# Buffers that are 32 bytes longer, and a smaller scratch for software DMAs, in a two-layer hybrid encoder on one core

## The chip, the cores and the metric

The kernel runs on one core of one Trainium2 chip. The metric is the device time of one execution in microseconds (us). Three executions of the kernel before took 2349.69 us at the median, between 2348.4 and 2352.19 us. One further execution was recorded by the profiler; it took 2351.57 us, of which its trace covers 2349.8 us from the first to the last instruction.

## The reference

The reference computes two layers of an encoder on one sequence of 512 tokens with a model width of 1024, all in fp32:

```python
for l in range(DEPTH):                       # 2 layers
    xn = rmsnorm(x, norm1_g[l])
    h = xn @ w_in[l]
    (a_qkv, a_z, a_ab, b_q, ..., d_o) = jnp.split(h, offsets, axis=-1)
    y_a = gdn_mixer(a_qkv, a_z, a_ab, ...)   # gated DeltaNet
    y_b = diff_mixer(b_q, b_k, b_v, ...)     # differential attention
    y_c = swa_mixer(c_q, c_k, c_v, ...)      # windowed attention
    y_d = mlstm_mixer(d_q, d_k, d_v, ...)    # mLSTM
    ys = jnp.stack([y_a, y_b, y_c, y_d], axis=2)
    branch = jnp.einsum('bsnw,nwd->bsnd', ys, w_branch[l])
    gate = jax.nn.sigmoid(jnp.einsum('bsd,dne->bsne', xn, w_gate[l]))
    x = x + jnp.sum(gate * branch, axis=2) @ w_out[l]
    xn = rmsnorm(x, norm2_g[l])
    x = x + jnp.square(jax.nn.relu(xn @ w_mlp1[l])) @ w_mlp2[l]
return rmsnorm(x, final_norm_g)
```

The large products with `w_in`, `w_gate`, `w_branch`, `w_out`, `w_mlp1` and `w_mlp2` take most of the time of the matrix engine; the four mixers are many small operations.

## The kernel before

**Products in three passes.** Every large operand v is held as two fp32r tiles, hi (a rounded copy of v, made by ScalarE) and lo (v minus hi, made by VectorE); `split` (L221 to L223) does it for activations and `emit_split` (L282 to L294) for weights. A product is then three matmuls per 128-deep step: hi times hi, hi times lo, lo times hi. Such a group of three is called a triple below. Each matmul loads a block of 128 x 128 as its stationary operand and streams 256 or 512 columns of the other operand, the moving one, through it.

**Where the operands lie.** Tiles come from pools of equally long buffers that lie behind one another in SBUF. Three pools matter here.

- `bg` has 13 buffers of 8,320 bytes per partition (L142, 2080 fp32 words of which 2048 are used). It holds the normalized activations (`xh`, `xl`), the mixers' outputs (`yh`, `yl`), the merged branches (`mh`, `ml`), the hidden layer of the MLP (`hh`, `hl`), the weights of the last MLP product (`twh`, `twl`), unsplit MLP weights (`wq`) and most large tiles of the mixers.
- `wp` has three buffers of 4,096 bytes each for `wh` and for `wl`, the split weights (L288, L289), and two of 4,096 bytes for `wr`, the weights as they come from memory.
- `ar` has 26 buffers of 2,080 bytes for tiles of 512 words, `xsh` and `xsl` of the MLP among them.

The start addresses follow from the order in which the pools are laid out behind a 16,384-byte scratch for software DMAs at address 0. In remainders by 256 bytes, all buffers of `wh`, `wl` and `wr` start at 160. The `bg` buffers start at 224 (buffers 0, 2, 4, ..., 12) or at 96 (buffers 1, 3, ..., 11). The `ar` buffers start at 160, 192, 224, 0, 32 and so on, a step of 32 from one to the next. The last `bg` buffer ends 416 bytes below the end of what the kernel may use. Which `bg` buffer a tile gets follows from the order in which the pool's buffers come free in the program.

**The products' forms.** In `run_a` (L374) the weights are the moving operand, 256 columns wide, and the activations are stationary; it serves the projections (on `xh`, `xl`), the first three quarters of the output projection (on `mh`, `ml`) and the second MLP product M2 (on `hh`, `hl`). M2 takes one pair `hh`, `hl` through four items in a row, one for each 256 columns of the output: 4 x 16 triples or 192 matmuls. `tail_item` (L682) has the same form for the last group of M2, with its weights in `bg`. `run_b` (L400) and `run_b2` (L415) have the weights stationary and 512 columns of `xh`, `xl` or `yh`, `yl` moving. The first MLP product, `M1` (L790), has the weights stationary and 256 columns moving, of `xh`, `xl` in `bg` for some factors and of `xsh`, `xsl` in `ar` for the others. `wo_last` (L741) and `m1_first` (L781) are small variants.

**Order.** The large products form one stream of items in a fixed order. `Item.get` looks ahead: it issues loads of weights on SyncE's queue up to five entries ahead (`emit_dma`, 512 KB each), and splits one or more entries ahead. A driver mixes this stream on TensorE with the small products of the mixers in the stretches 150 to 860 us and 1310 to 2020 us; the MLPs run nearly alone in 860 to 1185 us and from 2020 us to the end.

**Software DMAs.** `late_consts` (L199 to L203) issues six casting DMAs for constants from GpSimd near the start; all other loads and stores named here go through hardware queues.

Of the kernel before, what the change touches and what calls it, by code (L numbers as in the profile page):

```python
# [11 lines left out]
F32R = mybir.dt.float32r  # L12
# [5 lines left out]
P = 128  # L18
# [95 lines left out]
def encoder(ctx: ExitStack, tc: tile.TileContext, a: dict, out: bass.AP, dbg: dict = None):  # L114
    nc = tc.nc
# [5 lines left out]
    wp = ctx.enter_context(tc.tile_pool(name="wp", bufs=3))  # L121
    sp = ctx.enter_context(tc.tile_pool(name="sp", bufs=8))
    ar = ctx.enter_context(tc.tile_pool(name="ar", bufs=NAR))
    bg = ctx.enter_context(tc.tile_pool(name="bg", bufs=NBG))
# [5 lines left out]
    def nm(s):  # L130
        cnt[0] += 1
        return f"{s}_{cnt[0]}"
# [6 lines left out]
        return t[:, :S], t[:, S:2 * S]  # L139

    def B(dt=F32, s="b", w=2048):
        return bg.tile([P, 2080], dt, tag="bg", name=nm(s))[:, :w]  # L142

    def B4(dt=F32, s="b"):
        return B(dt, s).rearrange("p (k c) -> p k c", k=4)
# [10 lines left out]
    def f(ap):  # L156
        return ap.bitcast(F32)
# [24 lines left out]
    def x_load(src, between=None):  # L182
        b = [B(s="x") for _ in range(2)]
        xs = [[b[tt // 2][:, (tt % 2) * DM + h * S:(tt % 2) * DM + (h + 1) * S] for h in range(2)] for tt in range(NT)]
        for tt in range(NT):
            for h in range(2):
                nc.sync.dma_start(xs[tt][h], src[tt * P:(tt + 1) * P, h * S:(h + 1) * S])
            if between is not None:
                between(tt)
        return xs, [t.rearrange("p (t c) -> p t c", t=2) for t in b]  # L190
# [46 lines left out]
    class Item:  # L237
# [6 lines left out]
        def get(self, k):  # L244
            i = self.i0 + k
            last = len(loads) - 1
            la = G['la'] if self.label[:2] in ("m1", "m2") else 1
            while ns_[0] <= min(i + la, last):
                stage(np_, ns_[0], emit_pre)
                emit_split(ns_[0])  # L250
                ns_[0] += 1
            stage(np_, min(i + 2 + la, last), emit_pre)
            stage(nd, min(i + 5, last), emit_dma)
            return wt.pop(i)
# [27 lines left out]
    def emit_split(i):  # L282
        w = loads[i]
        raw = w["src"]() if "src" in w else raws.pop(i)
        if "dest" in w:
            wh, wl = w["dest"]()
        else:
            wh = wp.tile([P, w["kt"], w["nc"]], F32R, tag="wh", name=nm("wh"))  # L288
            wl = wp.tile([P, w["kt"], w["nc"]], F32R, tag="wl", name=nm("wl"))  # L289
        n = w["kt"] // G["sp"]  # L290
        for k in range(0, w["kt"], n):
            act.copy(wh[:, k:k + n], raw[:, k:k + n])  # L292
            dve.tensor_tensor(wl[:, k:k + n], raw[:, k:k + n], f(wh[:, k:k + n]), op=ALU.subtract)  # L293
        wt[i] = (wh, wl)  # L294
# [228 lines left out]
    def build(l, L):  # L523
# [5 lines left out]
        def z_evac(hp):  # L529
            def evac(tp, bank):  # L530
                if hp == 0 and tp == 0:
                    L.zs = B(s="zs").rearrange("p (t c) -> p t c", t=NT)
                d = L.zs[:, 2 * tp:2 * tp + 2, hp * 256:(hp + 1) * 256]
                b3 = bank.rearrange("p (t c) -> p t c", t=2)
                act.activation(d, b3, AF.Tanh, scale=0.5)
                dve.scalar_tensor_tensor(d, d, 1.0, b3, op0=ALU.add, op1=ALU.mult)
                for u in range(2):
                    d4 = d[:, u].rearrange("p (h c) -> p h c", h=2)
                    pool.tensor_tensor(d4, d4, bmid(L.gnh[:, 0, :], 2), op=ALU.mult)
            return evac  # L540
# [1210 lines left out]
```

## Time and profile before

| | before |
|---|---|
| median of three executions | 2349.69 us |
| profiled execution, device time | 2351.57 us |
| its span in the trace | 2349.8 us |
| outside the span | 1.8 us |
| TensorE (PE) busy | 2285.3 us, 97%, 16,992 matmuls |
| weight load (PEld) busy | 2083.2 us, 89% |
| VectorE (DVE) busy | 1582.2 us, 67% |
| ScalarE (ACT) busy | 1187.5 us, 51% |
| GpSimd (POOL) busy | 747.6 us, 32% |
| granted TensorE clock, mean | 0.996 |

TensorE's busy time nearly fills the span, so the sum of the times that its instructions take is nearly the time of the kernel. The duration which the profile gives for one matmul overlaps with that of the next one, since matmuls are pipelined; the pace of a row of matmuls is read from the time between their starts, or from a window that begins and ends with a row of them. A window's matmul count includes those that are still in flight at its start, so that it is a few above the number that started in it. [...]

### The profile page before, as it was taken

How to read it: one execution, taken by the hardware profiler on the slowest of the kernel's cores; microseconds unless marked ns; L12 is line 12 of the kernel's file. 1: busy time of each engine (PE TensorE's matmuls, PEld its weight loads, DVE VectorE, ACT ScalarE, POOL GpSimd, SP SyncE). 2: the span in 40 equal slices, each digit the busy share in tenths (PEclk: the TensorE clock that was granted, in tenths of full speed). 3: DMA queues.
4: the chain of work that ended last, by engine and by line, in shares of the span. 5: the costliest groups of instructions: out<-in, count | busy, mean ns of one | idle time of the engine just before them, and what ended most of it. 6: DMA issues, size and time to landing. Idle time of an engine off the chain costs nothing. (4 is left out here: it accounts for less than half of the span.)

```text
span 2349.8 us, 43335 instructions
## 1 busy us (share of the span) xinstructions
PE 2285.3 (97%) x16992; PEld 2083.2 (89%) x16992; DVE 1582.2 (67%) x2988; ACT 1187.5 (51%) x2777; POOL 747.6 (32%) x806
## 2 busy tenths in 40 slices
PE   7999999999999999999999999999999999999998
PEld 6879987989888989999987799879898889899998
DVE  5774547685786477677767745587767854867775
ACT  4565444654665264344445654365546643534443
POOL 1135552132232134343200555412313310434341
PEclk9999999999999999999999999999999999999999
DMA  6322131222122523333323112321221234233322
GB/s 149 99 46 64 55 95 57 60 88 80 51 71 74 160 71 122 95 109 108 111 74 90 55 55 64 91 63 52 93 82 55 72 106 131 90 97 109 99 82 90
DMA packets 234779, 200.72 MB, mean 85 GB/s; under 512 B 31696, under 2 KB 223824, under 8 KB 234576
## 3 DMA queue, kind: packets, MB, share of 16 engines
q1 hardware_dynamic: 231408, 192.75, 27.5%
q10 hardware_dynamic: 2304, 4.20, 0.5%
q8 instruction: 133, 2.18, 0.4%
q0 software_dynamic: 864, 1.02, 0.2%
q14 instruction: 70, 0.57, 0.1%
HBM read 190.04 MB, written 8.39 MB: 84 GB/s over the span
## 5 line engine op out<-in xcount | busy, mean ns | idle before, releaser
L293 DVE TENSOR_TENSOR wl<-wr,wh 128x512 fp32r<-128x512 f32 x540 | 400.4, 762 | 183.4 <-ACT wh L292 176.1
L292 ACT CAST wh<-wr 128x512 fp32r<-128x512 f32 x540 | 317.0, 621 | 219.0 <-PE pd L436 59.2
L392 PE MATMUL pd<-wh,xh 128*128 128x256 f32 x960 | 279.4, 291 | 0.0
L393 PE MATMUL pd<-wl,xh 128*128 128x256 f32 x960 | 269.8, 281 | 0.0
L394 PE MATMUL pd<-wh,xl 128*128 128x256 f32 x960 | 269.4, 281 | 0.0
L394 PE MATMUL pd<-wh,hl 128*128 128x256 f32 x896 | 248.2, 277 | 0.0
L392 PE MATMUL pd<-wh,hh 128*128 128x256 f32 x896 | 248.0, 277 | 0.0
L393 PE MATMUL pd<-wl,hh 128*128 128x256 f32 x896 | 248.0, 277 | 0.0
L292 ACT CAST wh<-wq 128x512 fp32r<-128x512 f32 x196 | 115.3, 619 | 220.4 <-PE pd L394 94.0
L435 PE MATMUL pd<-xh,wh 128*128 128x512 f32 (+1 forms) x544 | 217.7, 401 | 0.5 <-ACT xh L222 0.5
L436 PE MATMUL pd<-xl,wh 128*128 128x512 f32 (+1 forms) x544 | 209.0, 384 | 1.8 <-DVE xl L223 1.6
L437 PE MATMUL pd<-xh,wl 128*128 128x512 f32 (+1 forms) x544 | 208.8, 384 | 0.0
L293 DVE TENSOR_TENSOR wl<-wq,wh 128x512 fp32r<-128x512 f32 x196 | 181.9, 962 | 13.4 <-ACT wh L292 13.3
L393 PEld LDWEIGHTS pd<-wl,xh 128*128 128x128 f32 x960 | 181.9, 189 | 1.4
L392 PEld LDWEIGHTS pd<-wh,xh 128*128 128x128 f32 x960 | 181.5, 189 | 1.4
L394 PEld LDWEIGHTS pd<-wh,xl 128*128 128x128 f32 x960 | 181.3, 189 | 0.2
L809 POOL TENSOR_TENSOR wq<-wq,wq 128x512 f32<-128x512 f32 x84 | 124.4, 1488 | 163.1 <-DVE wl L293 153.7
L393 PEld LDWEIGHTS pd<-wl,hh 128*128 128x128 f32 x896 | 168.2, 188 | 0.0
L394 PEld LDWEIGHTS pd<-wh,hl 128*128 128x128 f32 x896 | 168.2, 188 | 0.0
L392 PEld LDWEIGHTS pd<-wh,hh 128*128 128x128 f32 x896 | 168.1, 188 | 0.0
L677 DVE TENSOR_TENSOR x<-pd,x 128x512 f32<-128x512 f32 x124 | 85.1, 689 | 101.4 <-PE pd L394 101.4
L1011 POOL TENSOR_TENSOR r<-r,r 128x512 f32<-128x512 f32 (+1 forms) x28 | 35.5, 1266 | 325.8 <-DVE r L1010 185.9
(394 smaller groups left out, 6656.9 us busy)
## 6 DMA issues: line engine op xcount, KB each, us to landing
wr<-in_w_in SPq DMA_DIRECT2D x92, 512.0 KB
wr<-in_w_mlp SPq DMA_DIRECT2D x72, 512.0 KB
wr<-in_w_gate SPq DMA_DIRECT2D x64, 512.0 KB
wq<-in_w_mlp SPq DMA_DIRECT2D x56, 512.0 KB
wr<-in_w_branch SPq DMA_DIRECT2D x32, 512.0 KB
wr<-in_w_out SPq DMA_DIRECT2D x16, 512.0 KB
x<-in_x SPq DMA_DIRECT2D x16, 256.0 KB
gsd<-gs ACTq DMA_DIRECT2D x16, 256.0 KB
```

The costliest lines, as they stand in the source:

```text
L292: act.copy(wh[:, k:k + n], raw[:, k:k + n])
L293: dve.tensor_tensor(wl[:, k:k + n], raw[:, k:k + n], f(wh[:, k:k + n]), op=ALU.subtract)
L392: mm(o, th, wh[:, k4, :], start=(kt == 0 and tt % 2 == 0), stop=False)
L393: mm(o, th, wl[:, k4, :], start=False, stop=False)
L394: mm(o, tl, wh[:, k4, :], start=False, stop=(kt == kts - 1 and tt % 2 == 1))
L435: mm(o, w1_, xh[kt][:, sl], start=(kt == 0 and hi_ == 0), stop=False)
L436: mm(o, w1_, xl[kt][:, sl], start=False, stop=False)
L437: mm(o, w2_, xh[kt][:, sl], start=False, stop=last)
L677: dve.tensor_tensor(d, bank.rearrange("p (t c) -> p t c", t=2), d, op=ALU.add)
L809: pool.tensor_tensor(d[:, k:k + 2], x[:, k:k + 2], y[:, k:k + 2], op=op)
L1011: pool.tensor_tensor(v(t1), v(t1), v(t2), op=ALU.add)
```

## The change

Three places are edited. The buffers of `bg` become 2088 words (8,352 bytes) long, and those of `wh` and `wl` become 1032 words (4,128 bytes); of each the same 2048 or 1024 words are used as before. The scratch for software DMAs at the start of SBUF becomes 4,096 bytes instead of 16,384. The 19 longer buffers need 608 bytes more than before.

```diff
     def B(dt=F32, s="b", w=2048):
-        return bg.tile([P, 2080], dt, tag="bg", name=nm(s))[:, :w]
+        return bg.tile([P, 2088], dt, tag="bg", name=nm(s))[:, :w]
...
-            wh = wp.tile([P, w["kt"], w["nc"]], F32R, tag="wh", name=nm("wh"))
-            wl = wp.tile([P, w["kt"], w["nc"]], F32R, tag="wl", name=nm("wl"))
+            wh, wl = [wp.tile([P, 1032], F32R, tag=t, name=nm(t))[:, :1024].rearrange("p (k c) -> p k c", k=w["kt"])
+                      for t in ("wh", "wl")]
...
-    nc = bacc.Bacc("TRN2", target_bir_lowering=False, num_devices=1)
+    nc = bacc.Bacc("TRN2", target_bir_lowering=False, num_devices=1, dynamic_dma_scratch_size=4096)
```

After it, in remainders by 256 bytes, the three buffers of `wh` start at 160, 192 and 224, those of `wl` at 0, 32 and 64, and the `bg` buffers at 160, 192, 224, 0, 32 and so on, a step of 32 from one to the next. The `ar` buffers all move by the same amount and keep their steps. No instruction is added or removed, and no size of an operand changes.

## Rows read from the trace of the kernel before

**Rows 1.** The page's first part: busy time, share and instructions of each engine.
```profile
PE 2285.3 (97%) x16992; PEld 2083.2 (89%) x16992; DVE 1582.2 (67%) x2988; ACT 1187.5 (51%) x2777; POOL 747.6 (32%) x806
```
**Rows 2.** TensorE's longest waits: line, releaser, us in total, times, longest us.
```profile
PE pm L487 <- DVE nj L472: 15.9, 10, 8.9
PE pm L834 <- DVE wl L293: 5.7, 2, 2.9
```
**Rows 3.** Windows of the two MLPs: us, busy of PE, PEld, DVE, ACT, POOL, clock, DMA.
```profile
860.00:1185.00 325.00, 322.12 (x2753) 321.13 (x2752) 235.87 (x324) 143.69 (x260) 125.55 (x97) 0.99 0.33 103
...
2020.00:2345.00 325.00, 320.04 (x2719) 319.37 (x2717) 227.40 (x312) 136.66 (x247) 123.34 (x95) 0.99 0.30 95
```
**Rows 4.** Groups of TensorE's instructions by form: line, tiles, count, busy, mean ns.
```profile
L392 PE MATMUL pd<-wh,xh 128*128 128x256 f32 x960 | 279.4, 291 | 0.0
...
L392 PE MATMUL pd<-wh,hh 128*128 128x256 f32 x896 | 248.0, 277 | 0.0
...
L435 PE MATMUL pd<-xh,wh 128*128 128x512 f32 x480 | 198.7, 414 | 0.0
...
L832 PE MATMUL pm<-xsh,wh 128*128 128x256 f32 x448 | 126.1, 282 | 0.0
...
L406 PE MATMUL pd<-xh,wh 128*128 128x512 f32 x304 | 121.3, 399 | 0.0
...
L435 PE MATMUL pd<-yh,wh 128*128 128x512 f32 x256 | 104.8, 410 | 0.0
...
L832 PE MATMUL pm<-xh,wh 128*128 128x256 f32 x336 | 95.3, 283 | 0.0
...
L392 PE MATMUL pd<-wh,mh 128*128 128x256 f32 x192 | 53.3, 278 | 0.0
...
L718 PE MATMUL pd<-twh,hh 128*128 128x256 f32 x128 | 36.2, 283 | 0.0
```
**Rows 5.** TensorE's windows of M2, 192 matmuls each: us, PE busy, clock, DMA, GB/s.
```profile
888.53:910.34 21.81, 21.81 (x194) 1.00 0.33 97
2045.83:2068.44 22.61, 22.61 (x194) 1.00 0.30 94
...
2255.60:2278.21 22.61, 22.61 (x194) 1.00 0.34 112
2298.05:2319.83 21.78, 21.78 (x194) 1.00 0.45 138
```
**Rows 6.** TensorE's timeline in a fast and a slow window of M2: start, us, line.
```profile
902.18 0.28 PE L392 MATMUL pd<-wh,hh 128*128 128x256 f32 x1
...
902.52 0.28 PE L392 MATMUL pd<-wh,hh 128*128 128x256 f32 x1
...
2050.07 0.28 PE L392 MATMUL pd<-wh,hh 128*128 128x256 f32 x1
...
2050.43 0.28 PE L392 MATMUL pd<-wh,hh 128*128 128x256 f32 x1
```
**Rows 7.** TensorE's windows of `run_a` on xh (48 matmuls) and mh (192, 288).
```profile
554.67:560.11 5.44, 5.44 (x50) 1.00 0.06 9
572.78:578.43 5.65, 5.65 (x51) 1.00 0.44 134
802.30:824.06 21.76, 21.76 (x195) 1.00 0.33 97
1947.20:1981.28 34.08, 34.08 (x289) 1.00 0.32 101
```
**Rows 8.** TensorE's windows of M1 (24, 72, 24 matmuls) and `tail_item` (93).
```profile
1124.07:1126.89 2.82, 2.82 (x27) 1.00 0.00 0
1126.89:1135.41 8.52, 8.52 (x74) 1.00 0.01 2
1135.41:1138.24 2.83, 2.83 (x26) 1.00 0.17 43
2331.27:2342.34 11.07, 11.07 (x96) 1.00 0.23 84
```
**Rows 9.** TensorE's windows of products 512 columns wide, 12 matmuls each.
```profile
49.10:51.87 2.77, 2.77 (x13) 1.00 0.20 59
51.87:54.68 2.81, 2.81 (x14) 1.00 0.09 17
861.34:864.10 2.76, 2.76 (x13) 1.00 0.03 6
```
**Rows 10.** GpSimd's timeline around the software DMAs: start, us, line, idle before.
```profile
20.51 0.76 POOL L201 DMA_DIRECT2D c_identr<-in_ident  x1
...
23.40 0.54 POOL L201 DMA_DIRECT2D c_swnegr<-in_swneg  x1
36.33 0.96 POOL L551 MEMSET wr<- 128x1024 f32 x1 [12.39 <-DVE wl L293]
```
**Rows 11.** Line 201's DMAs, issue to landing, and the first reader of their constants.
```profile
DMA to landing us min/median/max: 2.8/3.7/6.0
...
L1264 PE MATMUL pm<-c_negr,c_identr x32: 389/448/503, 133.9 to 1462.2; 128*128 128x512 f32 x32
```

## The prediction

> **What bounds the kernel now.** The page's busy times come first: TensorE is busy for 2285.3 of 2349.8 us, and no other engine is above 67% apart from the weight loads, which belong to TensorE [rows 1]. So the time is the sum of what TensorE's instructions take plus some 65 us in which it does nothing. Second, its waits: the largest kind sums to 15.9 us, the next to 5.7 us [rows 2], and the edit touches no wait. Third, the windows by stage: in both MLPs TensorE is busy for 322 of 325 and 320 of 325 us [rows 3]. What an edit of addresses can change is therefore the pace at which matmuls follow one another, and the transfers if these lost time. Fourth, the groups by form give the counts that a change of pace is multiplied with [rows 4]; their mean durations overlap and are no pace.
>
> The pace I read from windows that hold nothing but one row of matmuls. M2 gives the cleanest case: one pair hh, hl, 192 matmuls of 128x256, or 64 triples, and there are 896/64 = 14 such windows. Eleven take 21.76 to 21.82 us, three take 22.61 us [rows 5]; two of each kind are shown. The granted clock is 1.00 in all of them, TensorE has no gap, and the share of DMA is as high in a quick one (0.45) as in a slow one (0.34). The starts show the same step by step: 902.18 to 902.52 us is 340 ns for a triple, 2050.07 to 2050.43 us is 360 ns, about the 353 ns that 22.61/64 gives [rows 6]. Following the order in which bg's buffers are handed out, the three slow windows are those in which both hh and hl lie in odd buffers, at 96 by 256 bytes; in the eleven quick ones at least one of them starts at 224. The weights start at 160 in all. So the pace hangs on where the operands begin. The projections agree: with xh, xl in buffers 11 and 10, 48 matmuls take 5.44 us (340 ns a triple), with 9 and 1, both odd, 5.65 us (353 ns) [rows 7]. The offsets are not the whole story: the output projection ran at 340 ns in layer 0 (21.76/64) and at 355 ns in layer 1 (34.08/96) with hi odd and lo even in both [rows 7].
>
> [...]
>
> **The change part by part.** No instruction, wait, queue entry or size is added or removed. What moves is where wh, wl and bg begin against each other. Before, a weight buffer and a bg buffer always differ by 64 more than a multiple of 128 bytes (160 against 224 or 96). Afterwards wh at 160, 192, 224, wl at 0, 32, 64 and bg in steps of 32 differ by 0, 32, 64 or 96 by 128 about equally often, and wh and wl differ among themselves. Only one relation in four is the present one. For the other three the trace of before has two near rows. The weights of `tail_item` lie in bg as its activations do, so that they differ by 0 by 128: 11.07 us for 31 triples is 357 ns, in the form of `run_a` [rows 8]. And xsh, xsl in ar already stand in steps of 32 against the weights: M1 on them takes 8.52/24 = 355 ns, beside 2.82/8 = 352.5 and 2.83/8 = 354 ns with the same weights and xh in bg [rows 8]. No row of M1 shown reaches 340, with either pool. I price a triple afterwards at 3/4 x 355 + 1/4 x 340 = 351 ns. The ends are 340 (the quickest row of its width) and 357 (the slowest of these); I take a value near the upper end because both rows with another relation lie there.
>
> - *M2, 896 triples [rows 4].* Now 11 x 21.79 + 3 x 22.61 = 307.5 us. Afterwards 896 x 0.351 = 314.5 us: +7.0. Ends: 896 x 0.340 = 304.6 (-2.9) and 896 x 0.357 = 319.9 (+12.4).
> - *`run_a` on xh and mh, 960 + 192 = 1152 triples [rows 4].* The four windows give 340, 353, 340 and 355 ns [rows 7], 347 at equal weight. Afterwards 351: 1152 x 4 ns = +4.6. Ends: 1152 x (340 - 347) = -8.1 and 1152 x (357 - 347) = +11.5. In the stretch with the mixers the stream shares TensorE with small products, but TensorE is busy there too, so a slower triple lengthens the stretch by itself.
> - *M1, 448 + 336 = 784 triples, and the tail, 128 [rows 4].* They stand at 352.5 to 357 ns now [rows 8] and stay there: 0. Ends: 912 x (340 - 355) = -13.7 and 912 x 2 ns = +1.8.
> - *512 columns, 480 + 304 + 256 = 1040 triples [rows 4].* Four triples take 2.76, 2.77 or 2.81 us [rows 9], 690 to 702 ns a triple; the windows do not favour a relation, since 2.77 and 2.81 stand in one item. Taken as 0, with the middle of the rows at 695 as what holds before and after. Ends: 1040 x (690 - 695) = -5.2 and 1040 x 7 ns = +7.3.
> - *Small products of the mixers.* Their operands move by the same steps. They are short and most wait for other engines, and no row tells them apart by address: 0, inside the ends above.
> - *VectorE, ScalarE, GpSimd.* They read and write the moved buffers too, but have at least 33% of idle time [rows 1]; in the MLP window VectorE is busy 235.87 of 325 us and GpSimd 125.55 [rows 3]. Nothing of them is late next unless they slow by a third.
> - *The smaller scratch.* Its users are six DMAs that GpSimd issues between 20.51 and 23.94 us, one every 0.5 us without waiting for a landing of 2.8 to 6.0 us [rows 10, 11]. Afterwards 0 at best. At worst each issue waits for the landing before it, 6 x 6.0 = 36 us instead of 3.4, so that GpSimd is free at 56.5 instead of 23.9 us; 12.39 us of that lie in the idle time ahead of the memset at 36.33 us, which comes 20 us late [rows 10]. The constants' first reader comes at 133.9 us [rows 11], so they would land in time, and only the memsets behind them on GpSimd would be late. I take 0.
>
> **The sum.** 7.0 + 4.6 + 0 = 11.6 us on the profiled execution of 2351.57 us, whose span is 2349.8 us: 2363.2 us. The median of the runs is 1.9 us below the profiled one, so on the median it is 2349.7 + 11.6 = 2361 us. With all lower ends: -2.9 - 8.1 - 13.7 - 5.2 = -30 us, 2320 us. With all upper ends: 12.4 + 11.5 + 1.8 + 7.3 = +33 us, 2383 us.
>
> **The rivals.**
>
> *A. Nothing to measure, 2350 us.* Either the pace hangs on something other than addresses, such as what ran just before, or gains in one place pay for losses in another; in both cases the mean paces stay and the time with them. For it: two windows with the same offsets ran at 340 and 355 ns [rows 7], so something else has a say. Against it: the three slow windows of M2 are just those with both operands at 96 [rows 5], and no other engine's work sets them apart. [...]
>
> *B. Faster, 2335 us.* [...] Its place is `run_a`, 2048 triples, now (307.5 + 1152 x 0.347)/2.048 = 345 ns in the mean. At 340 ns M2 gains 2.9 and xh and mh 8.1 us; if the 336 triples of M1 on bg join at 340, another 336 x 12.5 ns = 4.2 us: 2349.7 - 15.2 = 2335 us. It decides once the mean of `run_a` falls below 343 ns (2048 x 2.3 ns = 4.7 us), which asks for more than four in five triples at 340 ns with the rest at 355. For it: half of the windows of `run_a` shown have the slow pace at the present offsets, so these are not the best possible [rows 5, 7]. Against it: every row with another relation stands at 355 or 357 [rows 8].
>
> *C. The scratch delays GpSimd, 2358 us.* The 20 us above, less than half of which TensorE would feel, since its stream of large products runs beside the mixers: +8. Against it: 3.4 us for six issues, far apart from their landing [rows 10, 11].
>
> **How the numbers follow.** The three runs spread by 3.8 us, so that about 0.2%, or 4.7 us, is what can be told from no change. The forecast (slower by run_a's pace, 2355 to 2383 us) has 0.48, A 0.24, B 0.26, C 0.02. Slower by over 0.2%: 0.48 + 0.02 = 0.50; within: 0.24; faster: 0.26. Both signs hold a good part, so the forecast's own range stands apart: 2355 to 2377 us. The range of 8 in 10 runs from 2338 us, which leaves out B's further half with some 0.11, to 2377 us, which leaves out the highest sixth of the forecast, 0.08.
>
> **What the changed profile would show.** If the forecast holds, M2's fourteen windows are no longer mostly 21.8 us but 22.5 us in the mean, the first MLP's window grows by some 5 us and the second's, which holds the three slow ones, by 2 us, and M1's rows stand where they did. By A the fourteen windows keep three at 22.6 us, or change one against another. By B nearly all stand at 21.8 us and the windows on xh at 5.44 us. By C the issues of line 201 lie several us apart, and the first memset of GpSimd starts after 40 us. The prediction is wrong if the two rows off the present relation, ar and tail, owe their pace to something else than their offsets (that M1 has the weights stationary, for one): then 340 ns may be as common as now or commoner, and the gain of B is on.

## The result: 0.67% slower

The changed kernel takes 2366.69 us at the median, beside 2350.94 us for the kernel before in the same runs: +15.8 us, ratio 1.0067, 95% interval 1.0049 to 1.0084. The forecast was 2361 us, with a range of 2338 to 2377 us. Its profiled execution took 2367.07 us with a span of 2365.3 us.

The first part of the page after, which answers [rows 1] (busy us, share of the span, instructions):

```profile
PE 2302.6 (97%) x16992; PEld 2100.7 (89%) x16992; DVE 1580.2 (67%) x2988; ACT 1187.5 (50%) x2777; POOL 748.2 (32%) x806
```

TensorE does the same 16,992 matmuls and is busy 2302.6 - 2285.3 = 17.3 us longer; the span grew by 15.5 us. DVE, ACT and POOL did the same work in nearly the same time. TensorE's longest waits after, which answer [rows 2]:

```profile
PE pm L487 <- DVE nj L472: 15.7, 8, 9.2
PE pm L834 <- DVE wl L293: 5.5, 2, 2.7
```

Nothing new waits. So the pace of the matmuls is what moved. TensorE's windows of M2 after (192 matmuls each, the first two and two late ones of fourteen), then the two of the output projection (288 each); the columns are us, PE busy, granted clock, DMA share and GB/s:

```profile
890.11:912.71 22.60, 22.60 (x195) 1.00 0.27 83
932.50:955.23 22.73, 22.73 (x194) 1.00 0.28 88
2185.29:2208.14 22.85, 22.85 (x194) 1.00 0.27 87
2312.92:2335.53 22.61, 22.61 (x194) 1.00 0.44 133
790.21:824.28 34.07, 34.07 (x290) 1.00 0.33 103
1959.37:1993.26 33.89, 33.89 (x289) 1.00 0.33 104
```

Beside [rows 5] no window of 21.8 us is left: all fourteen take 22.60 to 22.85 us at a clock of 1.00. In the output projection, where [rows 7] have 21.76 us for 192 matmuls or 340 ns a triple in layer 0, 34.07/96 is 355 ns. The projections on xh lost their quick windows as well; two of them after, 48 matmuls each:

```profile
554.63:560.32 5.69, 5.69 (x50) 1.00 0.33 94
571.68:577.38 5.70, 5.70 (x51) 1.00 0.42 132
```

They stand at 356 ns a triple; the two in [rows 7] took 5.44 and 5.65 us, 340 and 353 ns.

The whole can be summed from the starts of the matmuls in the two traces. The table gives the mean time of a triple from its first start to the start of the next one, over those triples into which no other matmul or wait came. The difference multiplies it with all triples of the row. For run_a on xh, xl only two thirds of the triples are undisturbed, with 512 columns about half, so that these rows are estimates.

| products | triples in the kernel | before, ns | after, ns | difference |
|---|---|---|---|---|
| M2 on hh, hl | 896 | 343.2 | 354.6 | +10.2 us |
| run_a on xh, xl | 960 | 347.5 | 354.0 | +6.2 us |
| run_a on mh, ml | 192 | 347.6 | 353.9 | +1.2 us |
| M1 on xh / on xsh | 336 / 448 | 353.0 / 354.8 | 353.7 / 354.7 | +0.2 us |
| tail | 128 | 355.8 | 354.5 | -0.2 us |
| 512 columns: L406 xh / L435 xh / L435 yh | 304 / 480 / 256 | 694.0 / 695.0 / 696.0 | 694.3 / 695.2 / 694.0 | -0.3 us |

The sum is +17.3 us, as much as TensorE's busy time grew by; that they meet to the tenth is chance, since two rows are estimates and small groups are left out. Afterwards every form stands at 354 ns, or at 694 ns with 512 columns.

### The profile page after: what moved, and what is told of

Its sections match the earlier page's. It is cut to its first block, busy times and chain, and to the rows that moved or that the text cites. A ratio compares the mean times of both kernels' runs of the same rounds, so it can differ in the third digit from the quotient of the medians.

```text
span 2365.3 us, 43337 instructions
## 1 busy us (share of the span) xinstructions
PE 2302.6 (97%) x16992; PEld 2100.7 (89%) x16992; DVE 1580.2 (67%) x2988; ACT 1187.5 (50%) x2777; POOL 748.2 (32%) x806
## 4 chain that ended last, share of the span: by engine, by line
PE 84%; DVE 7%; ACT 3%; POOL 3%; issue 2%; DMA 0%; SPq 0%; POOLq 0%; DVEq 0%; ACTq 0%
PE pd L392 9%; PE pd L393 9%; PE pd L394 9%; PE pd L435 7%; PE pd L436 7%; PE pd L437 7%; PE pm L834 4%; PE pm L833 4%; PE pm L832 4%; PE pd L407 2%; PE pd L406 2%; PE pd L408 2%; PE pm L1561 1%; DVE wl L293 1%; POOL r L1011 1%
## 5 line engine op out<-in xcount | busy, mean ns | idle before, releaser
L435 PE MATMUL pd<-xh,wh 128*128 128x512 f32 (+1 forms) x544 | 217.2, 400 | 0.5 <-ACT xh L222 0.5
L293 DVE TENSOR_TENSOR wl<-wq,wh 128x512 fp32r<-128x512 f32 x196 | 179.7, 951 | 15.5 <-ACT wh L292 15.5
```

The source lines that it names most:

```text
L435: mm(o, w1_, xh[kt][:, sl], start=(kt == 0 and hi_ == 0), stop=False)
```

## The experiments

Ratios are against the kernel before in the same runs; its median there was between 2351.1 and 2352.5 us.

### Which of the three edits costs

Only bg longer, with the smaller scratch that makes the room (`e1_bg`):

```diff
-        return bg.tile([P, 2080], dt, tag="bg", name=nm(s))[:, :w]
+        return bg.tile([P, 2088], dt, tag="bg", name=nm(s))[:, :w]
...
+    nc = bacc.Bacc("TRN2", target_bir_lowering=False, num_devices=1, dynamic_dma_scratch_size=4096)
```

> bg buffers of 8,352 bytes and the smaller scratch; wh and wl stay as before, all six at 160 by 256 bytes, while bg goes in steps of 32. Theory (the pace hangs on how weights and activations begin against each other, and only a difference of 64 by 128 bytes gives 340 ns a triple): one bg buffer in four keeps that difference, so M2 and the projections go most of the way to 354 ns; about 3/4 of the whole change's +16 us, 2359 to 2366 us. Rival 1 (the steps among the weight buffers are what costs): 2350 us as before. Rival 2 (the scratch): as e3.

Measured: 2368.89 us, ratio 1.0068 (1.0053 to 1.0083), all of the loss and not three quarters. M2's windows, the first two and the last:

```profile
892.34:914.95 22.61, 22.61 (x194) 1.00 0.26 83
934.81:957.83 23.02, 23.02 (x194) 1.00 0.27 87
2315.88:2338.11 22.23, 22.23 (x195) 1.00 0.44 138
```

One window of fourteen is below 22.6 us and none at 21.8. That one buffer in four keeps its old relation to the weights helps little, since hh and hl have to keep it at once: in the small kernel below (`micro1`) of the 64 rows in which xh and xl go through all steps of 32, just one reached 340 ns.

Only wh and wl longer, with a filler behind them that leaves bg at 224 and 96 (`e2_w`):

```diff
+    pool.memset(sp.tile([P, 16], F32, tag="fill", name="fill", bufs=1), 0.0)
...
+            wh, wl = [wp.tile([P, 1032], F32R, tag=t, name=nm(t))[:, :1024].rearrange("p (k c) -> p k c", k=w["kt"])
+                      for t in ("wh", "wl")]
```

> wh and wl of 4,128 bytes (wh at 160, 192, 224, wl at 0, 32, 64 by 256 bytes); bg stays at 224 and 96, scratch as before; a filler of 64 bytes keeps bg there. Theory: the differences to bg are now mixed, wl and wh never both at 64 by 128, so M2 stands at 354 ns in most windows: 2362 to 2368 us, all of the change's loss. Rival 1 (the steps among bg buffers are what costs): 2350 us. Rival 2 (the scratch): 2350 us.

Measured: 2368.61 us, ratio 1.0071 (1.0056 to 1.0086), at the theory's upper end. M2's triples stand at 355.1 ns, those on xh at 355.0; its first and last window:

```profile
889.07:911.89 22.82, 22.82 (x195) 1.00 0.30 93
2313.39:2336.01 22.62, 22.62 (x194) 1.00 0.43 135
```

A load's wh and wl lie in buffers of the same number, so that here and in the change itself wl begins 96 bytes above wh by 256 in every triple (160 and 0, 192 and 32, 224 and 64). In `micro1` the eight rows with wl at 96 took 353.2 to 356.8 ns: as far as they go, no start of the activations makes up for that. Each of the two edits costs by itself what both cost together, as a state does that either spoils, not a sum.

Only the smaller scratch (`e3_scratch`):

```diff
+    nc = bacc.Bacc("TRN2", target_bir_lowering=False, num_devices=1, dynamic_dma_scratch_size=4096)
```

> Only the scratch is smaller, 4,096 bytes; every tile moves down by 12,288 bytes, a multiple of 256, so all offsets by 256 stay. Theory: the same as before, 2350 us within 0.2%, M2 windows of 21.8 us eleven times and 22.6 three times. Rival (the scratch delays GpSimd, or the absolute address counts beyond its remainder): 2355 to 2367 us.

Measured: 2350.26 us, ratio 0.9993 (0.9984 to 1.0003): no difference. Two windows of M2, and the output projection of layer 0:

```profile
888.87:910.68 21.81, 21.81 (x194) 1.00 0.30 97
2044.86:2067.47 22.61, 22.61 (x194) 1.00 0.30 94
790.21:824.44 34.23, 34.23 (x289) 1.00 0.32 98
```

All fourteen windows of M2 have the length that they had before, the quick and the slow ones each in its place, although every tile lies 12,288 bytes lower. The third line is the exception: with the same remainders by 256 it took 34.23 us, where the kernel before has this row for the whole of it (the last 192 matmuls of it stand in [rows 7]):

```profile
791.39:824.06 32.67, 32.67 (x290) 1.00 0.36 109
```

So the remainders alone don't fix the pace. hi starts 192 bytes above the weights by 256 and lo 64 in this row, an offset at which `micro2` below finds both paces.

### The pace by itself

A kernel of nothing but rows of matmuls on one SBUF tile (`micro1`). Each row has its own starts of wh, wl, xh and xl, counted in bytes from the start of wh, and four short matmuls part it from the next. Abridged, with the operands' names of the encoder:

```python
for i in range(32):                                   # the form of run_a
    k, s = i % 4, blk((i // 4) % 4)
    mm(o, xh[:, k, s], wh[:, k], ...)
    mm(o, xh[:, k, s], wl[:, k], ...)
    mm(o, xl[:, k, s], wh[:, k], ...)
CELLS = [("a", 0, 0, d, d) for d in range(0, 1024, 32)] + ...
```

> It leaves the whole encoder out and writes copies of x. TensorE runs rows of triples on one SBUF tile, each row with other start offsets: 32 rows with wh = wl = 0 and xh = xl at 0 to 992 in steps of 32 bytes (32 triples each, the form of run_a), 64 rows with xh and xl apart, 64 with wl and x apart, 64 of the form of M1 (24 triples), 64 of 512 columns (12 triples). Theory: in the form of run_a 340 ns a triple where weights and activations differ by 64 by 128 bytes (8 of the first 32 rows) and 354 ns elsewhere; the other forms have quick offsets too or stand at 353 to 355 and 694 ns throughout. Rival (offsets alone do nothing; it is the other engines' traffic or what ran before): all rows of one form at one pace.

Measured: windows of 32 triples in the form of run_a, xh = xl at 64, 320, 32 and 0 bytes from the start of the weights:

```profile
82.92:94.30 11.38, 11.38 (x99) 1.00 0.00 0
177.72:188.70 10.98, 10.98 (x98) 1.00 0.01 1
71.20:82.55 11.35, 11.35 (x99) 1.00 0.01 1
59.25:70.72 11.47, 11.47 (x98) 1.00 0.01 1
```

In the second half of a window the steps are regular: 353.3, 340.0, 354.9 and 360.0 ns a triple. No other engine was at work in them, and the clock is 1.00. The pattern repeats every 256 bytes (from 256 on, the three rows with the same remainder agree within 0.2 ns: 340.0 at 320, 576 and 832; 353.3 at 448, 704 and 960; 350.3 at 480, 736 and 992). But 64 and 320 are one remainder and took 353.3 and 340.0. Of all 192 rows of 256 columns with wh at 0 and other mixtures of starts in steps of 32, two reached 340.0, one 347, and all others stood between 350 and 363. Of the eight rows from which the theory expected 340 ns, three reached it: offsets do set the pace, but by 256 bytes and not by 128 (320 gave 340.0, 192 and 448 gave 353.3), and 64 does not always give 340.

The entry into a row was varied next (`micro2`): the parting matmuls are 64, 88, 112 or 136 columns wide, and the order is shuffled.

```diff
-        for k in range(4):
-            mm(ps[7][:, :64], ...)
+        for k in range(4):
+            mm(ps[7][:, :cur[0]], ...)
...
+    for c in (64, 88, 112, 136):
+        CELLS.extend([("a", 0, k, i, j, c) for k in R for i in R for j in R])
```

> It leaves the whole encoder out, as micro1 did. All 64 offsets (wl, xh, xl) in steps of 64 bytes with wh = 0, four times each in the form of run_a (32 triples), and 16 offsets (xh, xl), four times each, in the forms of M1 and of 512 columns; the order is shuffled, and the matmuls that part two rows are 64, 88, 112 or 136 columns wide, so that each offset is entered in four ways. Theory (offsets decide): the four entries of one offset agree, and those with xh and xl at 64 or 192 and wl at 0 stand at 340 ns, those at 0 or 128 at 360. Rival (the entry decides, the offsets only say which paces there are): entries of one offset differ, with 340 ns in some and 353 in others.

Measured: two neighbouring rows at the very same addresses (wh = wl = 0, xh = xl = 64), then the four entries of xh = 64, xl = 192, a quick and a slow entry of xh = 192, xl = 64, and a row of 512 columns (12 triples) with equal starts:

```profile
692.44:703.42 10.98, 10.98 (x98) 1.00 0.01 1
703.82:715.18 11.36, 11.36 (x98) 1.00 0.00 0
933.85:944.80 10.95, 10.95 (x98) 1.00 0.01 1
1573.41:1584.38 10.97, 10.97 (x98) 1.00 0.01 1
1867.08:1878.08 11.00, 11.00 (x99) 1.00 0.01 1
4082.43:4093.42 10.99, 10.99 (x98) 1.00 0.01 1
1039.63:1050.62 10.99, 10.99 (x99) 1.00 0.01 1
1916.21:1927.70 11.49, 11.49 (x98) 1.00 0.01 1
1743.90:1752.13 8.23, 8.23 (x38) 1.00 0.01 2
```

Both were partly right. At 64, 64 one entry in four settles at 340.0 ns and three at 353.3: the offset allows more than one pace, and the addresses alone do not choose between them. At 64, 192 all four settle at 340.0. At 192, 64 two settle at 340.0 and two at 356.5 to 356.9, and at 192, 192 one at 340.0 and three at 353.3. This fits the kernel before: its three slow windows of M2, with hh and hl both at 96, are at 192, 192 and took 353 ns a triple, and the output projection of layer 0, at 192, 64, took 340 ns there and 356.6 in e3. In the form of run_a only four of the 64 offsets reached 340 in any entry: all had wl = wh, and x at 64 or 192. With 512 columns xh = xl at the start of the weights took 680.0 ns in all four, the others 687 to 704. M1's form reached 340 only at xh = xl = 192, in three of four. Equal starts, the best with 512 columns, are among the worst in the form of run_a (360.0 ns in all four entries; the slowest offset took 362.9).

### From the offsets to the kernel

All bg buffers at 224, so that they differ from the weights by 64 everywhere (`e4_all64`):

```diff
-        return bg.tile([P, 2080], dt, tag="bg", name=nm(s))[:, :w]
+        return bg.tile([P, 2112], dt, tag="bg", name=nm(s))[:, :w]
...
+    nc = bacc.Bacc("TRN2", target_bir_lowering=False, num_devices=1, dynamic_dma_scratch_size=4096)
```

> bg buffers of 8,448 bytes (33 x 256) with the smaller scratch and wh, wl as before: all thirteen bg buffers start at 224 by 256 bytes and all weights at 160, so that every product of weights with activations of bg has a difference of 64. Theory (a difference of 64 allows the 340 ns pace): all fourteen windows of M2 and all of the projections at 340 ns instead of eleven and about half; M2 gains 2.4 us, xh and mh some 1116 x 7.5 ns = 8 us: 2342 us. Rival (what ran just before decides between 340 and 353 ns at the same offsets, as the rows of micro1 at 64 show): the windows fall either way, between 2342 and 2362 us, and two with the same offsets differ.

Measured: 2342.43 us, ratio 0.9963 (0.9951 to 0.9976). The first window of M2 in each layer:

```profile
884.06:905.83 21.77, 21.77 (x194) 1.00 0.33 97
2037.38:2059.16 21.78, 21.78 (x195) 1.00 0.31 97
```

All fourteen take this time, and both output projections stand at 340.2 ns a triple. The projections on xh came to 344.9 ns instead of 340, some of their rows at 340 and some at 353 with the same offsets, as the rival had it; products of 512 columns, not in the expectation, fell from 695 to 689 ns. They make up for each other, so that it was luck that the time met the theory's 2342 us.

The same with a filler ahead of bg, so that the difference is 32 everywhere (`e7_all32`):

```diff
+    pool.memset(sp.tile([P, 56], F32, tag="fill", name="fill", bufs=1), 0.0)
```

> As e4 (all bg buffers at one remainder by 256, all weights at 160), but a filler of 224 bytes puts bg at 192, so that weights and activations differ by 32 everywhere. Theory (the relation decides): run_a at about 355 ns, the pace of micro1's row at 32: M2 +10 us and xh, mh +8 us against before, about 2368 us. Rival (it counts that all buffers of a pool begin alike, whatever the relation): 2342 us like e4.

Measured: 2368.98 us, ratio 1.0073 (1.0058 to 1.0088), and M2 at 355.0 ns, micro1's 354.9 at 32:

```profile
889.96:912.68 22.72, 22.72 (x195) 1.00 0.30 94
2057.16:2079.89 22.73, 22.73 (x194) 1.00 0.30 93
```

Two kernels that differ by a filler stand 27 us apart (2342.43 and 2368.98 us). It isn't how evenly the buffers begin, but by how much weights and activations differ.

The 512-column products with equal starts as well, by letting their weights begin 64 bytes later in longer buffers (`e6_b`):

```diff
+            o = w["off"]                 # 16 words for run_b and run_b2, else 0
+            wh, wl = [wp.tile([P, 1088], F32R, tag=t, name=nm(t))[:, o:o + 1024].rearrange("p (k c) -> p k c", k=w["kt"])
+                      for t in ("wh", "wl")]
```

> As e4, but the weight buffers are 256 bytes longer and the weights of the 512-column products begin 64 bytes later in them, at 224 as bg does, which is the row of micro2 that took 680 ns in all four entries; run_a keeps its difference of 64. Theory: the 1040 triples of 512 columns go from about 689 ns (e4) to 680: -9 us, 2333 us. Rival (between the mixers' small products the rows are too short for a pace to hold): 2340 to 2343 us like e4.

Measured: 2341.93 us, ratio 0.9960 (0.9945 to 0.9975), the rival's time but not for the rival's reason. The 512-column triples did fall, to 682.0, 686.6 and 685.6 ns, 1040 x 4.0 ns, about 4 us against e4. But M2 has a slow window and both output projections are slow; one of each:

```profile
2038.22:2060.83 22.61, 22.61 (x194) 1.00 0.30 94
786.02:819.95 33.93, 33.93 (x290) 1.00 0.34 104
```

Their addresses by 256 are those of e4; what runs ahead of them is not. The output projections lose 192 x 13.1 ns = 2.5 us and M2 0.9 us by it, and two small groups that got the same shift or the same entry (the 256-column halves of the first gate, the last quarter of the output projection) 1.3 us. So the losses add up to 4.7 us and eat the gain; the 0.5 us by which the two medians differ are far within the intervals of the two ratios.

A start for each form (`e5_forms`): bg and ar all at 160, weights 64 below them for run_a and the tail, equal for 512 columns, 192 below for M1.

```diff
+OA, OB, OM, OT = 48, 0, 16, 48           # words: run_a, 512 columns, M1, tail
...
-        return ar.tile([P, 516], dt, tag="ar", name=nm(s))[:, :w]
+        return ar.tile([P, 576], dt, tag="ar", name=nm(s))[:, :w]
...
-                    v = lambda t: t.rearrange("p k c -> p (k c)")[:, (i % 2) * 1024:(i % 2) * 1024 + 1024] \
+                    v = lambda t: t[:, OT + (i % 2) * 1024:OT + (i % 2) * 1024 + 1024] \
```

> Each form gets its own start: activations in bg and in ar all at 160 (ar buffers of 2,304 bytes), weights 64 below them for run_a and the tail, equal for 512 columns, 192 below for M1 (the rows of micro2 that reached 340, 680 and 340 ns). Theory, all at these paces: against before M2 and run_a -10, M1 784 x 14 ns = -11, tail -2, 512 columns 1040 x 15 ns = -15: 2313 us at best. Rival (the entry decides in part, so M1 and the projections reach it only in some stretches): 2320 to 2335 us.

Measured: 2341.09 us, ratio 0.9952 (0.9935 to 0.9969), above the rival's range. The tail fell from 355.8 to 340.1 ns, but M1 stayed at 352.6 and 352.0 and the output projections at 353.3. These and the other rows that the trace resolves, summed as in the table above, fell by some 18 us against before, while TensorE's busy time fell by 8.6 us (2276.7 after 2285.3). Some 5 us of that gap may be the clock (an estimate: a mean granted clock of 0.994 in this profiled execution and 0.996 in that of before, 0.002 x 2341 us); the rest is not resolved. The first two windows of M2 and the first output projection:

```profile
885.25:907.87 22.62, 22.62 (x194) 1.00 0.29 90
927.66:949.44 21.78, 21.78 (x194) 1.00 0.29 91
785.98:819.90 33.92, 33.92 (x289) 1.00 0.34 106
```

Same offsets, 22.62 and 21.78 us: the choice that 64, 64 leaves. It is also the offset of e4, which had all fourteen windows quick with bg at 224 and the weights at 160; here they are at 160 and 96, and twelve are quick. So the difference gave quick windows at either place, and e4's fourteen out of fourteen were in part luck. The next step takes that choice away, with hl and ml 128 bytes later (`e8_lo`):

```diff
     def B4(dt=F32, s="b"):
-        return B(dt, s).rearrange("p (k c) -> p k c", k=4)
+        o = 32 if s in ("hl", "ml") else 0
+        return B(dt, s, 2112)[:, o:o + 2048].rearrange("p (k c) -> p k c", k=4)
```

> e5 with one more step: hl and ml begin 128 bytes later in their buffers, so that in M2 and the output projection hi differs from the weights by 64 and lo by 192, the offset of micro2 that gave 340 ns in all four entries, where 64 and 64 gave it in one. Theory (the offset decides how often a row ends in the quick pace; what ran before only chooses where the offset leaves a choice): the mh windows, at 353 ns in e5, and all of M2 at 340: -2.5 and -2.0 us against e5, 2336 to 2338 us. Rival (what ran before decides alone): as e5, 2341 us, with mh at 353.

Measured: 2335.75 us, ratio 0.9925 (0.9909 to 0.9942). The same first window of M2 and output projection:

```profile
883.33:905.14 21.81, 21.81 (x195) 1.00 0.31 97
...
786.42:819.09 32.67, 32.67 (x289) 1.00 0.35 109
```

All fourteen windows of M2 (340.6 ns) and both output projections (340.3) are quick, as the theory had it and not the rival. By itself this would not decide, since e4 had all of them quick at 64, 64; but e9 below, with the same offsets in M2 and the output projection, has all sixteen quick once more.

M1's form was then looked at over all offsets (`micro3`):

```diff
-        CELLS.extend([("a", 0, k, i, j, c) for k in R for i in R for j in R])
-        CELLS.extend([(f, 0, 0, i, j, c) for f in "mb" for i in R for j in R])
+        CELLS.extend([(f, 0, k, i, j, c) for f in "mb" for k in R for i in R for j in R])
```

> It leaves the whole encoder out, as micro2 did: all 64 offsets (wl, xh, xl) in steps of 64 bytes with wh = 0, four entries each, for the forms of M1 and of 512 columns. Theory: a few offsets give 340 and 680 ns in all four entries, as 64, 192 did in the form of run_a and 0, 0 with 512 columns; most stand between 350 and 360 and between 687 and 700. Rival (M1's form has no quick pace of its own): no offset of it gives 340 in all four.

Measured: two of the 64 offsets of M1's form settled at 340.0 ns in all four entries, xh = xl = 192 with wl at 0 or at 128. With 512 columns only equal starts gave 680. The windows of wl = 128 (24 triples, the first of which have not settled):

```profile
297.70:305.95 8.25, 8.25 (x75) 1.00 0.00 0
1830.68:1838.98 8.30, 8.30 (x75) 1.00 0.00 0
3639.19:3647.48 8.29, 8.29 (x74) 1.00 0.01 2
4055.31:4063.53 8.22, 8.22 (x74) 1.00 0.00 0
```

The offset with wl at 0 is the one that M1 has in e5 and e8 without being quick there, and that had a slow entry in micro2. So the other was tried (`e9_m1`):

```diff
+            d = 32 if o == OM else 0
...
+                      for t, q in (("wh", o), ("wl", o + d))]
```

> e8 with the lo weights of M1 128 bytes further: wl - wh = 128 and x - wh = 192, which took 340.0 ns in all four entries of micro3. Theory (an offset that is quick in every entry is quick in the kernel too): M1's 784 triples go from 353 to 340 ns, -10 us against e8, 2326 us. Rival (M1's short rows of 8 triples, with new operands after each, don't settle, as (0, 192, 192) didn't in e5 and e8): 2336 us like e8.

Measured: 2325.61 us, ratio 0.9892 (0.9874 to 0.9909), 1.1% below the kernel before and 41 us below the change. M1 stands at 340.8 and 340.1 ns. Its window of 24 triples on xsh, first in e8, then in e9:

```profile
2233.18:2241.66 8.48, 8.48 (x75) 1.00 0.59 187
```

```profile
2221.66:2229.82 8.16, 8.16 (x75) 1.00 0.59 185
```

## Why the prediction was right, point by point

- **The bound.** The time did follow the pace of the matmuls: TensorE's busy time grew by 17.3 us and the span by 15.5. No wait took over.
- **M2, +7.0 us.** It measured +10.2 (896 x 11.4 ns); the fourteen windows came to 22.70 us in the mean, where the forecast had 22.5. The direction held, and where the operands start was the cause (27 us between e4 and e7); the step that was mis-sized is the price of 351 ns. It let one relation in four keep 340 ns, but a triple has two weights and two activations, and all of them bear on the pace (in micro2 only four of the 64 offsets reached 340 in any entry, all with wl = wh and both activations at 64 or 192): wl stood 96 bytes above wh in every triple, and no window of fourteen was quick after. At 355 ns for all, the term would have been +10.6. Relations were counted by 128 bytes, and micro1 shows that the pattern goes by 256. (The bg buffers after the change stand 160 bytes apart by 256, since 8,352 is 32 x 256 + 160, and not 32; the eight remainders are the same in another order.) The rows from ar and the tail had the right price, in part by luck: the ar row is of M1's form, for which other offsets are quick (at 64, 192 it took 351.5 to 353.4 ns in micro2 where the form of run_a took 340.0). What the two forms have in common is that nearly all offsets stand between 350 and 363 ns.
- **run_a on xh and mh, +4.6 us.** It measured 6.2 + 1.2 = +7.4, by the same price; the 347 ns of before was right (347.5 and 347.6), in part by luck, since four windows at equal weight stood for 1152 triples.
- **M1, tail and 512 columns, 0.** They moved by 0.2, -0.2 and -0.3 us. The bounds toward gains were real, but not at these offsets: e9 has M1 at 340 ns and e6 the 512 columns at 682 to 687.
- **VectorE, ScalarE, GpSimd, 0.** Their busy times moved by -2.0, 0.0 and +0.6 us; nothing of theirs became late.
- **The scratch, 0.** e3 has a ratio of 0.9993. In the trace after, the last of the six issues starts at 23.49 us and the memset behind them at 36.35 us; [rows 10] have 23.40 and 36.33. With that rival C (the scratch delays GpSimd) is out:

```profile
23.49 0.54 POOL L201 DMA_DIRECT2D c_swnegr<-in_swneg  x1
36.35 0.96 POOL L551 MEMSET wr<- 128x1024 f32 x1 [12.32 <-DVE wl L293]
```

- **The sum, +11.6 us.** The medians moved by +15.8, so that the forecast was 4 us short of it. The two terms of M2 and run_a alone were 6.0 us short (17.6 us by the table, 11.6 forecast); the span grew by 1.8 us less than TensorE's busy time.
- **Rival A** (something other than addresses) is out as the cause of the change: e4 and e7 differ by a filler and by 27 us. What spoke for it was right all the same: at one address a row can take 340 or 353 ns. In micro2 no other engine was at work, DMA stood at 0.00 and 0.01, and two rows at the same addresses took 10.98 and 11.36 us. The example that the prediction gave for it was read too simply: the output projection of layer 1 has hi in an odd and lo in an even buffer, as in layer 0, in half of its triples only; in the other half both are odd. Its first two rows of 48 matmuls are one of each kind. The first (192, 192 from the weights) took 353 ns a triple and the second (192, 64) 356 ns, the slow paces of micro2 at these offsets:

```profile
1947.20:1952.85 5.65, 5.65 (x49) 1.00 0.23 69
1952.85:1958.55 5.70, 5.70 (x50) 1.00 0.50 162
```

- **Rival B** (faster, 2335 us) failed on its condition: the mean of run_a, which had to fall below 343 ns, came to 354 ns by the table above; no window of M2 or of the output projection stood at 340 after, and of the 192 mixed rows of micro1 two did. Its prize was there, for offsets chosen on purpose: the 15.2 us that it named were surpassed by e8 (-17) and e9 (-25), though in part by rows that it did not count, of 512 columns and of M1 on xsh.

Why some offsets are quick and others slow stays open. In the windows of the small kernels no other engine was at work and DMA stood at 0.00 or 0.01, so that neither sets the paces there apart; no run here tests a cause. What chooses between two paces at one offset stays open: no run here varied the entry alone, and in e3 the same instructions as in the kernel before run ahead of the output projection of layer 0, with another pace after them.

## What to carry to other kernels

Before padding buffers apart, look in the trace whether equal rows of matmuls run at different paces, and compare where their operands start: here that was worth 1.8% between the worst and the best arrangement (2368.98 and 2325.61 us), with the same 16,992 matmuls. Spreading the starts was the wrong cure; a fixed difference, chosen for each form of product and kept by buffer strides that are multiples of 256 bytes, was the right one. Choose the difference by a small kernel that enters each candidate from several states, and take one that is quick in all of them, then confirm it in the kernel, since M1's first such offset was not quick there (352.6 and 352.0 ns in e5).

## What the runs showed of the hardware

- A triple of 128x256 fp32r matmuls settles at a steady pace that differs from row to row, at a granted clock of 1.00: 340.0, 346.7, 353.3 and 360.0 ns come back exactly, others lie between 350 and 363; with 512 columns 680.0, 686.7, 693 and 700 ns come back, up to 707 (micro1, micro2 and micro3).
- Which of them are open depends on where the operands start by 256 bytes (in micro1 rows 256 bytes apart agree within 0.2 ns, but for 64 bytes, where two are open); where two are open, a row can take the one or the other at the very same addresses (340.0 and 353.3 ns in micro2).
- What suits one form does not suit another: equal starts gave the best pace with 512 columns (680.0) and one of the worst in the form of run_a (360.0 of at most 362.9 ns, micro2).
